# Hybrid attention layer on one core: a new order for loading, transposing and first using the token tiles

## The chip, the core and the metric

The kernel runs on 1 core of one Trainium2 chip. The metric is the device time of one execution in microseconds (us). Engines are named as in the profile: PE (TensorE matmul), PEld (its weight load), DVE (VectorE), ACT (ScalarE), POOL (GpSimd), SP (SyncE, which here only issues DMAs).

## What is computed

One layer over 512 tokens of width 1024, in float32. The index path, which the change touches first, decides for each query which 128 keys it may see.

```python
xn = rms_norm(h, norm_gain[l])
proj = xn @ w_in[l]
(q_a, k_a, v_a, g_a, q_i, k_i, w_i, c_q, c_kv, k_rope, g_b) = jnp.split(proj, offsets, axis=-1)
...
rel = jax.nn.relu(jnp.einsum('bqhd,bsd->bqhs', qib, k_idx).astype(jnp.float32))
score = jnp.einsum('bqhs,bqh->bqs', rel, wb.astype(jnp.float32)) * idx_scale
_, sel = lax.top_k(score, topk)
...
mixed = jnp.concatenate([o_a.reshape(B, S, A_WIDTH) * jax.nn.silu(g_a),
                         o_b.reshape(B, S, B_WIDTH) * jax.nn.silu(g_b)], axis=-1)
h = h + mixed @ w_out[l]
```

With 128 keys to keep, the first 128 queries see all the keys they may see, so index queries are needed for token tiles 1, 2 and 3 only.

## The kernel before

The 512 tokens are four tiles of 128. All matrix products run on pairs of tiles, a rounded part (names with h: `xh`, `wh`, `swh`) and the rest (`xl`, `wl`, `swl`), three products to a step (`mm3`, L178; recorded at L124). PE's order is written out by hand (`manual_schedule`, L88). The order on DVE, ACT, POOL and SP is made by the framework's scheduler.

The start. SP loads the four token tiles into `xin` (L196), two at a time, with the identity `ident` and three gain rows (`grow`, a `tmp` tile in the trace; L205 to L208) between them, then the small weights `smw` (L200, L201), 104 columns that make the index keys, head weights and rotary key. Per tile, ACT and DVE sum squares (L339, L340), DVE adds (L341), POOL takes the power -1/2 (`rsqrt`, L216), DVE scales the tile in place (L346). `x_turn` (L354) transposes on PE into PSUM banks and, once both tiles of a pair are in, ACT writes `xh` (L366) and DVE `xl` (L369), 256 tokens at a time. The pairs are (0, 1), then (2, 3).

Then PE makes the small projection in the bank `sm_acc` in two halves of 256 tokens (`small_step`, L476), and the index queries `q_i` of tiles 1, 2, 3 as a skewed stream (L482) woven into the second half. `use_small` (L420) turns the small projection to token-major and makes the index keys `kih`, `kil`. The latent projection `c_kv` follows, with the index scores (`sc<-kih,qi`) woven in from its tenth step on.

Weights come in chunks of 128 rows (`chunk`, L257): a DMA into one of 3 buffers `wst` (L259), a rounding copy `wh` on ACT (L263), a subtraction `wl` on POOL or DVE (L266; a string of letters such as "PPPD" says which). A chunk's DMA waits until the buffer is free, so until the `wl` three chunks earlier is done. SP issues in order. Eight counters (`DMAHW0` to `DMAHW7`) report landings and are used in turn, so an issue also waits for the landing of the DMA that was issued eight before it.

Eight small loads (`cs32`, `wide`, `gcol`, `gb`, `ga`; L487 to L492) stand in SP's order between the third and the fourth weight chunk.

Of the kernel before, what the change touches and what calls it, by code (L numbers as in the profile page):

```python
# [9 lines left out]
F32 = mybir.dt.float32  # L10
F32R = mybir.dt.float32r
# [5 lines left out]
D = 1024  # L17
# [27 lines left out]


AHEAD = 8
BANKS = {"mm": 3, "tr": 2, "sc": 2, "pv": 1}

LAG_KI = 7500  # L50
# [32 lines left out]
def layer(ctx: ExitStack, tc: tile.TileContext, x, norm_gain, w_in, a_q_norm, a_k_norm, b_q_latent,  # L83
# [21 lines left out]
    def psum(tag):  # L105
        return PS.tile([128, 512], F32, name=tag, tag=tag, bufs=BANKS[tag])

    def f32(ap):
        return ap.bitcast(F32)
# [17 lines left out]
    def transpose(o, i, idn):  # L127
        nc.tensor.transpose(o, i, idn)  # L128
        clock[0] += 107.0
# [19 lines left out]
    def run(g):  # L149
        for _ in g:  # L150
            tick()

    def take(g, n):
        for _ in range(n):
            if next(g, None) is None:
                return
            yield 1
# [20 lines left out]
    def mm3(o, lh, ll, rh, rl, first, last):  # L178
        matmul(o, lh, rh, first, False)
        matmul(o, lh, rl, False, False)  # L180
        matmul(o, ll, rh, False, last)
# [10 lines left out]
    wst = sb("qk8", (128, 8, 104), name="smw")  # L192
    wv = w_in.rearrange("(k p) c -> p k c", p=128)
    SWH, SWL = sb("V", (128, 8, 104), F32R, "swh"), sb("V", (128, 8, 104), F32R, "swl")
    for t in range(NT):
        nc.sync.dma_start(xin[t // 2][:, t % 2], xv[:, t])  # L196
        if t == NT - 1:
            for a in range(0, 8, 4):
                ks = slice(a, a + 4)
                nc.sync.dma_start(wst[:, ks, 0:32], wv[:, ks, 3272:3304])  # L200
                nc.sync.dma_start(wst[:, ks, 32:104], wv[:, ks, 2560:2632])  # L201
                nc.scalar.copy(SWH[:, ks], wst[:, ks])
                nc.gpsimd.tensor_tensor(SWL[:, ks], wst[:, ks], f32(SWH[:, ks]), op=OP.subtract)
        if t == 1:
            nc.sync.dma_start(ident, cst[:, 768:896])  # L205
            nc.sync.dma_start(grow[0:8], norm_gain.rearrange("(k p) -> k p", p=128))
            nc.sync.dma_start(grow[8:11], b_q_latent.rearrange("(k p) -> k p", p=128))
            nc.sync.dma_start(grow[11:13], b_kv_latent.rearrange("(k p) -> k p", p=128))  # L208

    nhalf = P.tile([128, 8], F32, name="nhalf")  # L210
    nc.gpsimd.memset(nhalf, -0.5)
# [6 lines left out]

    copies, subs, used = [], [], [0]

    def first(ins, m):

        for c in copies[used[0] + 1 + m:]:
            tc.add_manual_dep(c.ins, ins.ins.name, mybir.DependencyInfo(
                mybir.DependencyClass.NoSync, mybir.DependencyReason.DATA), reason="order")

    plan, where, done = [], {}, []
    IN = {"q_a": 0, "k_a": 512, "v_a": 1024, "g_a": 1536, "q_i": 2048, "g_b": 3304}
# [1 line left out]
    def weight(name, eng="P", high="A"):  # L230


        part = None
        if "/" in name:
            name, part = name.split("/")
        if name in IN:
            w, k0, k1, c, n = w_in, 0, 8, IN[name], 512
        elif name == "c_q":
            w, k0, k1, c, n = w_in, 0, 8, 2632, 384
        elif name == "c_kv":  # L240
            w, k0, k1, c, n = w_in, 0, 8, 3016, 256
        elif name[:3] == "ukv":
            w, k0, k1, c, n = w_ukv, 0, 2, 512 * int(name[3]), 512
        elif name[:2] == "uq":
            w, k0, k1, c, n = w_uq, 0, 3, 384 * int(name[2]), 384
        else:
            k0, k1 = {"ob": (4, 8), "oa": (0, 3), "oz": (3, 4)}[name[:2]]
            w, c, n = w_out, 512 * int(name[2]), 512
        ks = list(range(k0, k1))
        if part:  # L250
            a, b = part.split(":")
            ks = ks[int(a):int(b)]
        for i, k in enumerate(ks):
            where[name, k - k0] = len(plan)
            plan.append((w, k, c, n, eng[i % len(eng)], high[i % len(high)]))
# [20 lines left out]
            done.append(chunk(*plan[len(done)]))  # L276
        return done[j]

    weight("q_i", "PPPD")
    weight("c_kv", "P")  # L280
    weight("c_q", "D")
    for n in ("g_b/0:2", "ukv0", "g_b/2:3", "uq0", "g_b/3:5", "ukv1", "g_b/5:6", "uq1", "g_b/6:8"):
# [24 lines left out]
    def stream(jobs, group=2, banks=("mm",), skew=True):  # L307

        order, start = [], 0
        for i, (nk, _, _) in enumerate(jobs):  # L310
            s = start if skew else start - start % nk
            order += [(s + k, i, k) for k in range(nk)]
            start += nk / group
        acc = {}
        for _, i, k in sorted(order):
            nk, step, use = jobs[i]
            if k == 0:
                acc[i] = psum(banks[i % len(banks)])
            step(acc[i], k)
            if k == nk - 1:  # L320
                use(acc.pop(i))
            yield 1
# [6 lines left out]
    def xh(k):  # L329
        return XH[k // 4][:, k % 4]  # L330

    def xl(k):
        return XL[k // 4][:, k % 4]

    for t in range(NT):
        xt = xin[t // 2][:, t % 2]
        r = small(4)
        sq = tmp(), tmp()
        nc.scalar.activation(sq[0], xt[:, 0:512], AF.Square, scale=D ** -0.5, accum_out=r[:, 0:1])  # L339
        nc.vector.tensor_tensor_reduce(sq[1], xt[:, 512:], xt[:, 512:], 1.0 / D, EPS, OP.mult, OP.add, r[:, 1:2])  # L340
        nc.vector.tensor_tensor(r[:, 2:3], r[:, 0:1], r[:, 1:2], op=OP.add)  # L341
        rsqrt(r[:, 3:4], r[:, 2:3])
        w = D // 2 if t == NT - 1 else D
        for a in range(0, D, w):
            xs = xt[:, a:a + w]
            nc.vector.tensor_scalar(xs, xs, r[:, 3:4], None, op0=OP.mult)  # L346
    gp = psum("pv")
    transpose(gp[:, :13], grow[:13], ident[:13, :13])
    nc.scalar.copy(gains, gp[:, :13])


    xb = {}

    def x_turn(t):  # L354
        hf = t // 2
        if t % 2 == 0:
            xb[hf] = [psum(b) for b in (("tr", "tr", "sc", "sc"), ("mm", "mm", "mm", "tr"))[hf]]
        for k in range(8):
            c = (k % 2) * 256 + (t % 2) * 128
            transpose(xb[hf][k // 2][:, c:c + 128], xin[hf][:, t % 2, k * 128:k * 128 + 128], ident)  # L360
        parts = lambda k: [xb[hf][k // 2][:, (k % 2) * 256:(k % 2) * 256 + 256]] + [
            f(k)[:, hf * 256:hf * 256 + 256] for f in (xh, xl)]
        for b in range(0, 8 if t % 2 else 0, 2):
            for k in (b, b + 1):
                p, h, l = parts(k)
                nc.scalar.activation(h, p, AF.Copy, scale=gains[:, k:k + 1])  # L366
            for k in (b, b + 1):
                p, h, l = parts(k)
                nc.vector.scalar_tensor_tensor(l, p, gains[:, k:k + 1], f32(h), op0=OP.mult, op1=OP.subtract)  # L369


    cs32 = P.tile([128, 2, NT, 32], F32, name="cs32")
# [96 lines left out]
    def lat_kv(_, a):  # L469
        latent(a, 11, ckv, ckvs, "pt2")  # L470

    for t in range(NT):
        x_turn(t)
    sm_acc = psum("pv")

    def small_step(hf, k):  # L476
        c = slice(hf * 256, hf * 256 + 256)
        mm3(sm_acc[:104, c], SWH[:, k], SWL[:, k], xh(k)[:, c], xl(k)[:, c], k == 0, k == 7)

    for k in range(8):  # L480
        small_step(0, k)
    qi_ = stream(tok_jobs("q_i", 8, xh, xl, 512, [1, 2, 3], lambda t, a: use_qi(t, a)), 3, skew=True)  # L482
    for k in range(8):
        small_step(1, k)
        run(take(qi_, 1))
        if k == 2:
            nc.sync.dma_start(cs32, cst[:, 512:768])  # L487
    nc.sync.dma_start(wide, cst[:, 896:1408])
    for i, (b, a) in enumerate(((b_q_norm, a_q_norm), (b_k_norm, a_k_norm))):
        nc.sync.dma_start(gcol[0:64, 1 + i:2 + i], b[0:64].rearrange("(p o) -> p o", o=1))  # L490
        nc.sync.dma_start(gb[:, i], rows(b, 96))
        nc.sync.dma_start(ga[:, i], rows(a, 64))  # L492
    use_small(None, sm_acc)

    HALF = slice(0, 64), slice(64, 128)
# [2 lines left out]
    def use_qi(t, a):  # L500
        q = tmp()
        q3 = q.rearrange("p (h d) -> p h d", h=8)
        m = tmp((128, 8, 32))
        first(nc.scalar.copy(q, a), KEEP_QI)
        rope_mul(q3[:, :, 0:32], m, q3[:, :, 0:32], cs32, t, 8, 32)
        nc.vector.tensor_tensor(q3[:, :, 0:32], q3[:, :, 0:32], m, op=OP.add)

        def turn():
            p = psum("tr")
            for h in range(4):  # L510
                transpose(p[:, tok(h)], q[:, tok(h)], ident)
            p3 = p.rearrange("p (h c) -> p h c", h=4)
            for u in range(2):
                nc.scalar.copy(QI[u][HALF[u], :, tok(t - 1)], p3[HALF[u]])
            for u in range(2):
                a, b = QI[u][HALF[u], :, tok(t - 1)], QI[u][HALF[1 - u], :, tok(t - 1)]
                nc.vector.tensor_tensor(b, p3[HALF[u]], f32(a), op=OP.subtract)
        later(LAG_QI, turn)

    run(qi_)  # L520
    with tc.issue_after(subs[-1].ins):
# [43 lines left out]
    rl = P.tile([128, 8], F32, name="rl")  # L565

    rlx = P.tile([128, 16], F32, name="rlx")
    epsc = P.tile([128, 1], F32, name="epsc")
    nc.gpsimd.memset(epsc, EPS)
    kr = P.tile([128, NT, 32], F32, name="kr")  # L570
    kb = P.tile([128, NT], F32, name="kb")

# [367 lines left out]
```

## Time and profile before

| | us |
|---|---|
| median of 3 runs (lowest, highest) | 350.75 (348.65, 354.21) |
| the profiled execution | 350.51 |
| span of its trace, first to last instruction | 348.4 |

Times in the rows are microseconds from the start of the span. What lies around the span is 350.51 - 348.4 = 2.1 us. "idle before" in brackets is how long the engine had nothing to do, and what it waited for.

### The profile page before, as it was taken

The numbers are of one execution on the slowest core, as the hardware profiler recorded it, in microseconds if no ns is written. First come the engines' busy times: TensorE is split into PE (matmuls) and PEld (weight loads), VectorE is DVE, ScalarE is ACT, GpSimd is POOL, SyncE is SP. The second block draws the span as 40 slices with busy tenths as digits, with TensorE's granted clock in tenths as the row PEclk, the third lists the DMA queues.
The fourth block names the chain that finished last, engine by engine and source line by source line (L and its number), as shares of the span: only waits on it lengthen the run. The fifth ranks groups of instructions, "written<-read, shape, count | busy, mean of one in ns | idle before, by whom it ended". The sixth has DMA issues, their size and how long they took to land.

```text
span 348.4 us, 5497 instructions
## 1 busy us (share of the span) xinstructions
PE 328.3 (94%) x1696; PEld 273.9 (79%) x1696; DVE 264.5 (76%) x633; ACT 219.5 (63%) x528; POOL 181.7 (52%) x194
## 2 busy tenths in 40 slices
PE   2999999999999999999999799999999699999995
PEld 2887787887787888788888688888887588887884
DVE  4926787769998496887989889687997378667556
ACT  4944658583657785878876689434427688888210
POOL 1645452268689994236514379439827436356000
PEclk9999999999999999999999999999999899999999
DMA  7753334134033233013210055426678306200006
GB/s 264 192 150 105 92 115 144 31 99 122 24 105 92 74 105 94 0 32 98 83 33 0 18 135 151 122 60 152 178 188 279 111 20 201 70 16 0 2 0 241
DMA packets 28806, 34.83 MB, mean 100 GB/s; under 512 B 5341, under 2 KB 16874, under 8 KB 28778
## 3 DMA queue, kind: packets, MB, share of 16 engines
q1 hardware_dynamic: 28778, 34.49, 34.7%
q8 instruction: 13, 0.21, 0.2%
q14 instruction: 15, 0.12, 0.1%
HBM read 27.14 MB, written 2.10 MB: 84 GB/s over the span
## 4 chain that ended last, share of the span: by engine, by line
PE 64%; DVE 15%; DMA 7%; ACT 6%; issue 4%; POOL 2%; SPq 1%; DVEq 0%; ACTq 0%; POOLq 0%
PE mm L124 37%; PE sc L124 12%; PE pv L124 6%; PE tr L128 5%; DMA wst<-in_w_in 4%; DVE acc L552 2%; DVE m L551 2%; PE mm L128 2%; PE tr L124 2%; DVE ob L897 2%; ACT wh L263 2%; DMA wst<-in_w_out 1%; ACT z L683 1%; DVE z L682 1%; DMA xin<-in_x 1%
## 5 line engine op out<-in xcount | busy, mean ns | idle before, releaser
L266 POOL TENSOR_TENSOR wl<-wst,wh 128x512 fp32r<-128x512 f32 (+2 forms) x79 | 97.3, 1238 | 64.9 <-ACT wh L263 63.3
L263 ACT CAST wh<-wst 128x512 fp32r<-128x512 f32 (+2 forms) x89 | 51.7, 586 | 40.4 <-DMA wst<-in_w_in 21.3
L124 PE MATMUL mm<-wh,xh 128*128 128x512 f32 x120 | 50.3, 419 | 0.0
L124 PE MATMUL mm<-wl,xh 128*128 128x512 f32 x120 | 47.6, 396 | 0.2 <-POOL wl L266 0.2
L124 PE MATMUL mm<-wh,xl 128*128 128x512 f32 x120 | 47.4, 395 | 0.0
L216 POOL TENSOR_TENSOR sml<-sml,nhalf 128x4 f32<-128x4 f32 (+2 forms) x28 | 32.1, 1147 | 24.7 <-ACT sml L799 13.1
L683 ACT ACTIVATE z<-z,sml 128x512 f32<-128x512 f32 (+1 forms) x64 | 35.8, 560 | 9.5 <-DVE sml L682 9.1
L690 POOL TENSOR_SCALAR z<-z,sml 128x512 f32<-128x512 f32 (+2 forms) x32 | 18.8, 588 | 41.0 <-DVE sml L686 41.0
L124 PE MATMUL mm<-xh,wh 128*128 128x512 f32 x80 | 33.4, 417 | 0.0
L124 PE MATMUL mm<-xl,wh 128*128 128x512 f32 x80 | 31.7, 396 | 0.0
L124 PE MATMUL mm<-xh,wl 128*128 128x512 f32 x80 | 31.6, 395 | 0.0
L124 PEld LDWEIGHTS mm<-wh,xl 128*128 128x128 f32 x120 | 22.6, 188 | 5.4
L551 DVE MAX8 m<-acc 128x8 f32<-128x512 f32 (+2 forms) x48 | 26.4, 551 | 0.0
L552 DVE MATCH_REPLACE8 acc<-m,acc 128x512 f32<-128x512 f32 (+2 forms) x48 | 26.0, 541 | 0.0
L124 PEld LDWEIGHTS mm<-wl,xh 128*128 128x128 f32 x120 | 22.7, 189 | 3.5 <-POOL wl L266 0.5
L124 PEld LDWEIGHTS mm<-wh,xh 128*128 128x128 f32 x120 | 22.6, 189 | 3.0
L413 DVE TENSOR_TENSOR pl<-tr,ph 128x512 fp32r<-128x512 f32 (+1 forms) x32 | 17.6, 549 | 7.2 <-ACT ph L412 7.1
L124 PE MATMUL sc<-kl,bhl 96*128 96x512 f32 (+3 forms) x96 | 20.0, 320 | 0.0
L412 ACT CAST ph<-tr 128x512 fp32r<-128x512 f32 (+1 forms) x32 | 15.2, 473 | 7.7 <-PE tr L128 7.2
L128 PE MATMUL tr<-ident,z 128*128 128x128 f32 x96 | 16.1, 277 | 3.6 <-ACT z L692 3.5
L682 DVE CUSTOM_DVE_ANT_0 z<-sc,wide,nqb 128x512 f32<-128x512 f32 (+3 forms) x32 | 17.2, 541 | 2.5 <-PE sc L124 1.6
L682 DVE CUSTOM_DVE_ANT_0 z<-sc,acc,nqa 128x512 f32<-128x512 f32 (+2 forms) x24 | 14.5, 612 | 5.9 <-PE sc L124 5.7
(213 smaller groups left out, 886.6 us busy)
## 6 DMA issues: line engine op xcount, KB each, us to landing
wst<-in_w_in SPq DMA_DIRECT2D x48, 256.0 KB, 2.7
wst<-in_w_out SPq DMA_DIRECT2D x16, 256.0 KB, 2.9
xin<-in_x SPq DMA_DIRECT2D x4, 512.0 KB, 4.2
k_a<-tmp SPq DMA_DIRECT2D x16, 128.0 KB, 3.3
ob<-in_x SPq DMA_DIRECT2D x8, 256.0 KB, 3.6
out<-ob SPq DMA_DIRECT2D x7, 256.0 KB, 2.0
wst<-in_w_in SPq DMA_DIRECT2D x8, 192.0 KB, 2.6
wst<-in_w_uq SPq DMA_DIRECT2D x6, 192.0 KB, 2.2
```

The lines of the kernel that those rows point to most:

```text
L124: nc.tensor.matmul(o, l, r, start=start, stop=stop)
L128: nc.tensor.transpose(o, i, idn)
L216: nc.gpsimd.tensor_tensor(dst, src, nhalf[:, :src.shape[-1]], op=OP.pow)
L263: copies.append(nc.scalar.copy(h, st))
L266: i = E(eng).tensor_tensor(l, st, f32(h), op=OP.subtract)
L412: nc.scalar.copy(h, p)
L413: return nc.vector.tensor_tensor(l, p, f32(h), op=OP.subtract)
L551: nc.vector.max(m, masks[t])
L552: dve[0] = nc.vector.match_replace(masks[t], m, masks[t], -3e38).ins
L682: dve[0] = nc.vector.tensor_tensor_reduce(z, sc[:, :n], mask(t), nq(h, t), 3e38, OP.add, OP.min, r[:, i:i + 1]).ins
L683: nc.scalar.activation(z, z, AF.Exp, bias=r[:, i:i + 1], scale=-1.0, accum_out=r[:, 2 + i:3 + i])
L690: nc.gpsimd.tensor_scalar(z, z, w, 0.0, op0=OP.mult, op1=OP.add)
```

## The change

The identity is loaded first, then the token tiles in the order 1, 2, 3, 0; the gain rows go out from ACT's queue. PE multiplies a tile of zeros 15 times before its first transpose. The pairs are now (1, 2) and (3, 0). After the first pair is transposed and split, PE makes the index queries of tiles 1 and 2, and after each of the first four chunks of `q_i` transposes one bank of the second pair. The small projection follows in one piece of 512 tokens, woven with the other four chunks of `q_i` for tiles 1 and 2. Tile 3's index queries come last, from the same eight chunks. The small weights are loaded after the first three weight chunks, and `wide` and the others after that. The sum of the two halves' squares is added on POOL, and every tile is scaled in two halves. Two chunks of `q_i` get their `wl` on DVE, as before, but the fifth and eighth (before: the fourth and eighth).

```diff
-    for t in range(NT):
-        nc.sync.dma_start(xin[t // 2][:, t % 2], xv[:, t])
...
+    PAIRS = (1, 2), (0, 3)
+    XIN = {t: xin[i][:, j] for i, ts in enumerate(PAIRS) for j, t in enumerate(ts)}
+    nc.sync.dma_start(ident, cst[:, 768:896])
+    for t in (1, 2, 3, 0):
+        nc.sync.dma_start(XIN[t], xv[:, t])
+    nc.scalar.dma_start(grow[0:8], norm_gain.rearrange("(k p) -> k p", p=128))
...
+    zero = tmp()
+    nc.vector.memset(zero, 0.0)
+    zr = zero.bitcast(F32R)
+    warm = psum("mm")
+    for _ in range(WARM):
+        nc.tensor.matmul(warm, zr[:, 0:128], zr, start=True, stop=True)
...
-    weight("q_i", "PPPD")
+    weight("q_i", "PPPPDPPD")
...
-        nc.vector.tensor_tensor(r[:, 2:3], r[:, 0:1], r[:, 1:2], op=OP.add)
+        nc.gpsimd.tensor_tensor(r[:, 2:3], r[:, 0:1], r[:, 1:2], op=OP.add)
...
+    for t in (1, 2):
+        x_scale(t)
...
+    for j in range(2):
+        for b in range(4):
+            x_turn(0, b, j)
+            if j == 1:
+                x_split(0, b)
+    for t in (3, 0):
+        x_scale(t)
...
-    for k in range(8):
-        small_step(0, k)
-    qi_ = stream(tok_jobs("q_i", 8, xh, xl, 512, [1, 2, 3], lambda t, a: use_qi(t, a)), 3, skew=True)
-    for k in range(8):
-        small_step(1, k)
-        run(take(qi_, 1))
...
+    q1 = stream(tok_jobs("q_i", 8, xh, xl, 512, [1, 2], lambda t, a: use_qi(t, a)), 2, skew=False)
+    for b in range(4):
+        run(take(q1, 2))
+        x_bank(1, b)
+        for j in (1, 0):
+            x_turn(1, b, j)
+        x_split(1, b)
+        if b == 0:
+            for a in range(0, 8, 4):
...
+            nc.sync.dma_start(cs32, cst[:, 512:768])
...
+    sm_acc = psum("pv")
+    for k in range(8):
+        mm3(sm_acc[:104], SWH[:, k], SWL[:, k], xh(k), xl(k), k == 0, k == 7)
+        run(take(q1, 1))
+    use_small(None, sm_acc)
+    qi_ = stream(tok_jobs("q_i", 8, xh, xl, 512, [3], lambda t, a: use_qi(t, a)), 1)
+    nc.sync.dma_start(wide, cst[:, 896:1408])
```

From the latent projection on, the order on every engine is the same in both kernels, but for a few neighbours that trade places. Before it, the order differs; three places follow.

On ACT, at the start, before (`xin_63` and `xin_64` each hold two token tiles, `xh_91` the first four and `xh_92` the last four blocks of 128 features):

```order
L339 ACTIVATE tmp,sml<-xin_63 128x512 x2
L349 COPY gains<-pv 128x13
L339 ACTIVATE tmp,sml<-xin_64 128x512 x2
L366 ACTIVATE xh_91<-tr,gains 128x256 x3
L202 CAST swh<-smw 128x416
...
L366 ACTIVATE xh_92<-sc,gains 128x256 x4
...
L263 CAST wh<-wst 128x512
```

and now (`xin_63` holds tiles 1 and 2, `xin_64` tiles 0 and 3):

```order
L350 ACTIVATE tmp,sml<-xin_63 128x512 x2
L350 ACTIVATE tmp,sml<-xin_64 128x512
L390 COPY gains<-pv 128x13
L350 ACTIVATE tmp,sml<-xin_64 128x512
L381 ACTIVATE xh_101<-tr,gains 128x256 x4
L271 CAST wh<-wst 128x512 x2
L381 ACTIVATE xh_102<-sc,gains 128x256 x4
L271 CAST wh<-wst 128x512
L381 ACTIVATE xh_101<-tr,gains 128x2x128 x2
L271 CAST wh<-wst 128x512
```

The squares of all four tiles still stand ahead of the first `xh`; the first `wh` moves up to right behind four of the first pair's eight `xh`.

On PE, now, from the first instruction to the third weight chunk:

```order
L212 MATMUL mm<-tmp 128x512 x15
L130 MATMUL pv<-ident,tmp 128x13
L130 MATMUL tr<-ident,xin_63 128x128 x4
L130 MATMUL sc<-ident,xin_63 128x128 x4
...
L126 MATMUL mm<-wh,xh_101 128x512
L126 MATMUL mm<-wl,xh_101 128x512
L126 MATMUL mm<-wh,xl_103 128x512
...
L130 MATMUL tr<-ident,xin_64 128x128 x4
```

Before, all 32 transposes and 12 steps of the small projection stood ahead of the first product with `wh`; now 16 transposes stand ahead of it, and the second of its three products needs `wl` at once.

On SP, now, from the first weight chunk to the fourth (with what each issue waits for):

```order
L267 DMA wst<-in_w_in 128x512 [waits DMAHW0_49]
L267 DMA wst<-in_w_in 128x512 [waits DMAHW1_49]
L267 DMA wst<-in_w_in 128x512 [waits DMAHW2_49]
L537 DMA smw<-in_w_in 128x4x32 [waits DMAHW3_49]
L538 DMA smw<-in_w_in 128x4x72 [waits DMAHW4_49]
...
L539 DMA cs_182<-cst 128x256 [waits DMAHW7_49]
L555 DMA wide<-cst 128x512 [waits DMAHW0_49]
L557 DMA gcol<-in_b_q_norm 64x1 [waits DMAHW1_49]
...
L559 DMA ga<-in_a_k_norm 128x64 [waits DMAHW6_49]
L267 DMA wst<-in_w_in 128x512 [waits DMAHW7_49,Pool_49]
```

The three chunks now go out behind the token tiles, and the four loads of `smw` stand between them and the fourth chunk together with the eight small loads; counter 3 is the landing of tile 3, counter 4 that of tile 0, the last.

## Rows read from the trace of the kernel before

**Rows 1.** The page: busy time by engine, and the chain that ended last.
```profile
PE 328.3 (94%) x1696; PEld 273.9 (79%) x1696; DVE 264.5 (76%) x633; ACT 219.5 (63%) x528; POOL 181.7 (52%) x194
...
PE 64%; DVE 15%; DMA 7%; ACT 6%; issue 4%; POOL 2%; SPq 1%; DVEq 0%; ACTq 0%; POOLq 0%
```

**Rows 2.** Timeline of PE, start to first index scores: start, us, engine, line, what.
```profile
6.93 1.11 PE L128 MATMUL tr<-ident,xin 128*128 128x128 f32 x4 [0.70 <-DVE xin L346]
...
13.66 0.36 PE L124 MATMUL pv<-xh,swh 128*104 128x256 f32 x1
...
16.93 0.40 PE L124 MATMUL mm<-wh,xh 128*128 128x512 f32 x1
17.17 0.39 PE L124 MATMUL mm<-wl,xh 128*128 128x512 f32 x1
...
19.62 0.51 PE L124 MATMUL mm<-wl,xh 128*128 128x512 f32 x1 [0.19 <-POOL wl L266]
...
34.93 0.63 PE L128 MATMUL tr<-ident,tmp 128*128 128x128 f32 x4 [0.51 <-DVE tmp L506]
...
38.21 0.60 PE L128 MATMUL tr<-ident,tmp 128*128 128x128 f32 x4
38.56 0.49 PE L124 MATMUL pv<-xh,wh 128*128 128x512 f32 x1
38.89 0.40 PE L124 MATMUL pv<-xl,wh 128*128 128x512 f32 x1
...
42.33 0.65 PE L128 MATMUL tr<-ident,tmp 128*128 128x128 f32 x4 [0.27 <-DVE kil L413]
...
47.03 0.40 PE L124 MATMUL sc<-kih,qi 128*128 128x512 f32 x1
```

**Rows 3.** Timeline of DVE: the first and the last token tile arrive.
```profile
4.10 0.69 DVE L340 CUSTOM_DVE_ANT_0 tmp<-xin 128x512 f32<-128x512 f32 x1 [4.10 <-DMA xin<-in_x]
...
9.15 0.69 DVE L340 CUSTOM_DVE_ANT_0 tmp<-xin 128x512 f32<-128x512 f32 x1 [0.50 <-DMA xin<-in_x]
```

**Rows 4.** Timeline of ACT and POOL: square, split, weight copy, weight subtraction.
```profile
9.23 0.63 ACT L339 ACTIVATE tmp<-xin 128x512 f32<-128x512 f32 x1 [1.23 <-DMA xin<-in_x]
...
9.86 1.18 ACT L366 ACTIVATE xh<-tr,gains 128x256 fp32r<-128x256 f32 x3
...
11.72 1.58 ACT L366 ACTIVATE xh<-sc,gains 128x256 fp32r<-128x256 f32 x4
...
18.98 0.62 ACT L263 CAST wh<-wst 128x512 fp32r<-128x512 f32 x1 [0.78 <-DMA wst<-in_w_in]
...
18.28 1.29 POOL L266 TENSOR_TENSOR wl<-wst,wh 128x512 fp32r<-128x512 f32 x1 [0.88 <-ACT wh L263]
```

**Rows 5.** Timeline of SP: the small weights, the eight small loads, the fourth chunk.
```profile
5.92 0.51 SPq L200 DMA_DIRECT2D smw<-in_w_in  x1
...
9.94 0.43 SPq L487 DMA_DIRECT2D cs<-cst  x1
...
13.85 0.33 SPq L492 DMA_DIRECT2D ga<-in_a_k_norm  x1
16.17 18.69 SPq L259 DMA_DIRECT2D wst<-in_w_in  x13
```

**Rows 6.** DMA issues of the first 20 us: KB each, us from issue to landing.
```profile
smw<-in_w_in SPq DMA_DIRECT2D x2, 144.0 KB, 4.7
```

**Rows 7.** PE after its longest later wait: timeline, then windows (PEclk: granted clock).
```profile
272.73 0.66 PE L128 MATMUL tr<-ident,z 128*128 128x128 f32 x4 [3.00 <-ACT z L692]
...
274.00:276.00 2.00, 2.00 (x9) 1.89 (x8) 0.57 (x3) 1.92 (x6) 1.22 (x2) 0.50 0.51 173
276.00:278.00 2.00, 2.00 (x8) 1.55 (x8) 1.11 (x3) 0.69 (x3) 0.00 (x0) 0.70 0.46 145
```

**Rows 8.** PEld: four transposes early and four late in the first stage.
```profile
7.62 0.87 PEld L128 LDWEIGHTS sc<-ident,xin 128*128 128x128 f32 x4
...
12.03 0.42 PEld L128 LDWEIGHTS mm<-ident,xin 128*128 128x128 f32 x4
```

More of the change, by code (lines that the diff above doesn't have):

```diff
@@ L47 @@
 AHEAD = 8
+WARM = 15
 BANKS = {"mm": 3, "tr": 2, "sc": 2, "pv": 1}
@@ L194, in layer @@
     SWH, SWL = sb("V", (128, 8, 104), F32R, "swh"), sb("V", (128, 8, 104), F32R, "swl")
-    for t in range(NT):
-        nc.sync.dma_start(xin[t // 2][:, t % 2], xv[:, t])
[L197 to L208, printed above, removed]
+    PAIRS = (1, 2), (0, 3)
[4 more added lines that the diff above has]
+    nc.scalar.dma_start(grow[0:8], norm_gain.rearrange("(k p) -> k p", p=128))
+    nc.scalar.dma_start(grow[8:11], b_q_latent.rearrange("(k p) -> k p", p=128))
+    nc.scalar.dma_start(grow[11:13], b_kv_latent.rearrange("(k p) -> k p", p=128))
+    zero = tmp()
[4 more added lines that the diff above has]
+        nc.tensor.matmul(warm, zr[:, 0:128], zr, start=True, stop=True)
     nhalf = P.tile([128, 8], F32, name="nhalf")
@@ L219, in layer, with after @@
     copies, subs, used = [], [], [0]
+    def after(v, u):
+        tc.add_manual_dep(v.ins, u.ins.name, mybir.DependencyInfo(
+            mybir.DependencyClass.NoSync, mybir.DependencyReason.DATA), reason="order")
     def first(ins, m):
         for c in copies[used[0] + 1 + m:]:
-            tc.add_manual_dep(c.ins, ins.ins.name, mybir.DependencyInfo(
-                mybir.DependencyClass.NoSync, mybir.DependencyReason.DATA), reason="order")
+            after(c, ins)
     plan, where, done = [], {}, []
@@ L333, in xl, with x_scale @@
         return XL[k // 4][:, k % 4]
-    for t in range(NT):
-        xt = xin[t // 2][:, t % 2]
+    epsc = P.tile([128, 1], F32, name="epsc")
+    nc.gpsimd.memset(epsc, EPS)
+    def x_scale(t):
+        xt = XIN[t]
         r = small(4)
@@ L340, in layer, with x_bank, x_turn, x_split @@
         nc.vector.tensor_tensor_reduce(sq[1], xt[:, 512:], xt[:, 512:], 1.0 / D, EPS, OP.mult, OP.add, r[:, 1:2])
-        nc.vector.tensor_tensor(r[:, 2:3], r[:, 0:1], r[:, 1:2], op=OP.add)
+        nc.gpsimd.tensor_tensor(r[:, 2:3], r[:, 0:1], r[:, 1:2], op=OP.add)
         rsqrt(r[:, 3:4], r[:, 2:3])
[L343 to L346, printed above, removed]
+        for a in (0, 512):
+            nc.vector.tensor_scalar(xt[:, a:a + 512], xt[:, a:a + 512], r[:, 3:4], None, op0=OP.mult)
+    xb, xsp = {}, {}
+    def x_bank(i, b):
+        if b == 0:
+            xb[i] = {}
+        xb[i][b] = psum(("tr", "tr", "sc", "sc")[b])
+    def x_turn(i, b, j):
+        for k in (2 * b, 2 * b + 1):
+            c = (k % 2) * 256 + j * 128
+            transpose(xb[i][b][:, c:c + 128], XIN[PAIRS[i][j]][:, k * 128:k * 128 + 128], ident)
+    def x_split(i, b):
+        def parts(k):
+            p = xb[i][b][:, (k % 2) * 256:(k % 2) * 256 + 256]
+            h, l = xh(k), xl(k)
+            if i == 0:
+                return p, h[:, 128:384], l[:, 128:384]
+            return [p.rearrange("p (j c) -> p j c", j=2)] + [
+                v.rearrange("p (t c) -> p t c", t=NT)[:, 0:NT:3] for v in (h, l)]
+        for k in (2 * b, 2 * b + 1):
+            p, h, l = parts(k)
+            xsp[i, b] = nc.scalar.activation(h, p, AF.Copy, scale=gains[:, k:k + 1])
+        for k in (2 * b, 2 * b + 1):
+            p, h, l = parts(k)
+            nc.vector.scalar_tensor_tensor(l, p, gains[:, k:k + 1], f32(h), op0=OP.mult, op1=OP.subtract)
+    for t in (1, 2):
+        x_scale(t)
     gp = psum("pv")
@@ L349, in layer @@
     nc.scalar.copy(gains, gp[:, :13])
[L352 to L357, printed above, removed]
-        for k in range(8):
[L359 to L369, printed above, removed]
+    for b in range(4):
+        x_bank(0, b)
+    for j in range(2):
[5 more added lines that the diff above has]
+        x_scale(t)
     cs32 = P.tile([128, 2, NT, 32], F32, name="cs32")
@@ L470, in lat_kv @@
         latent(a, 11, ckv, ckvs, "pt2")
[L472 to L478, printed above, removed]
-    for k in range(8):
-        small_step(0, k)
-    qi_ = stream(tok_jobs("q_i", 8, xh, xl, 512, [1, 2, 3], lambda t, a: use_qi(t, a)), 3, skew=True)
-    for k in range(8):
-        small_step(1, k)
-        run(take(qi_, 1))
[L486 to L493, printed above, removed]
     HALF = slice(0, 64), slice(64, 128)
@@ L518, in use_qi @@
         later(LAG_QI, turn)
+    q1 = stream(tok_jobs("q_i", 8, xh, xl, 512, [1, 2], lambda t, a: use_qi(t, a)), 2, skew=False)
+    for b in range(4):
+        run(take(q1, 2))
[3 more added lines that the diff above has]
+        x_split(1, b)
+        if b == 0:
+            for a in range(0, 8, 4):
+                ks = slice(a, a + 4)
+                nc.sync.dma_start(wst[:, ks, 0:32], wv[:, ks, 3272:3304])
+                nc.sync.dma_start(wst[:, ks, 32:104], wv[:, ks, 2560:2632])
+            nc.sync.dma_start(cs32, cst[:, 512:768])
+    for a in range(0, 8, 4):
+        ks = slice(a, a + 4)
+        c = nc.scalar.copy(SWH[:, ks], wst[:, ks])
+        after(c, xsp[1, 1])
+        i = nc.gpsimd.tensor_tensor(SWL[:, ks], wst[:, ks], f32(SWH[:, ks]), op=OP.subtract)
+    for v in copies[5:]:
+        after(v, c)
+    for v in subs[4:]:
+        after(v, i)
+    sm_acc = psum("pv")
[5 more added lines that the diff above has]
+    nc.sync.dma_start(wide, cst[:, 896:1408])
+    for i, (b, a) in enumerate(((b_q_norm, a_q_norm), (b_k_norm, a_k_norm))):
+        nc.sync.dma_start(gcol[0:64, 1 + i:2 + i], b[0:64].rearrange("(p o) -> p o", o=1))
+        nc.sync.dma_start(gb[:, i], rows(b, 96))
+        nc.sync.dma_start(ga[:, i], rows(a, 64))
     run(qi_)
@@ L567, in layer @@
     rlx = P.tile([128, 16], F32, name="rlx")
-    epsc = P.tile([128, 1], F32, name="epsc")
-    nc.gpsimd.memset(epsc, EPS)
     kr = P.tile([128, NT, 32], F32, name="kr")
```

## The prediction

> **What bounds the kernel now.** I read the page first. PE is busy 94% of the span and carries 64% of the chain that ended last [rows 1]: the kernel is a queue of products, so an edit pays when it brings PE's queue forward or takes a wait out of it. The change edits the time up to the latent projection, so next comes PE's timeline there [rows 2]. PE does nothing before 6.93 us. It transposes until 13.66, where the small projection starts, makes its first product with a weight at 16.93, the first of the latent projection at 38.56, the first index score at 47.03. After 13.66 it waits seldom: 0.35 us at 19.62, where a `wl` is late (19.27, one product after the last, would have been its turn), some 0.5 at 34.93, 0.27 at 42.33. So what the stage can give back lies before 13.66 and is about 7 us of transposing with waits in it.
>
> Since PE's, ACT's, DVE's and POOL's orders are practically equal in both kernels from the latent projection on, I compare two instants: the first product of the latent projection (38.56 before) and the first index score (47.03 before). A shift there goes through to the end, because PE stays the bound.
>
> **The work of PE between the first weight product and the latent projection.** Successive products of 512 columns start 0.235 us apart (16.93 to 17.17) [rows 2]. The changed order has 72 of them for the index queries and 24 for the small projection: 96 x 0.235 = 22.6. A group of four transposes among them costs 0.45: 0.35 to the next product (38.21 to 38.56) and 0.1 more until that one has passed (0.33 instead of 0.235, 38.56 to 38.89) [rows 2]. There are seven: four of the pair (3, 0), one of the small projection, two of index queries; 3.15. Together 25.7 us.
>
> **When the first weight product can start.** Tiles landed from 4.10 to 9.15 before [rows 3]. Four tiles of 512 KB still have to come, now with the identity ahead and no small weights queued right behind. I take 9.0 for the last one, tile 0, with ends of 8.6 and 9.5. The order of ACT decides the rest: the square of tile 0 stands ahead of the first `xh`, so no `xh` begins before about 9.0 + 0.63 = 9.63 [rows 4]. Four `xh` at 1.58 for four and one weight copy of 0.62 follow: the first `wh` is there at 9.63 + 1.58 + 0.62 = 11.8 [rows 4], and PE makes its first weight product at 11.8 instead of 16.93. Its second needs `wl`, 1.29 on POOL [rows 4]: there at 13.1, while PE would have had its turn at 12.05. A new wait of 1.05 us; behind it on PE stands everything, the transposes of tiles 3 and 0 too.
>
> **The fourth chunk.** After that wait PE needs 5 x 0.235 for the first chunk, 1.41 for each of the next two (POOL's 1.29 per chunk keeps pace) and 0.45 for each of three groups of transposes: 13.1 + 1.2 + 2.8 + 1.35 = 18.45, and the second product of the fourth chunk would have its turn at 18.7. Its DMA stands behind four loads of small weights, of which the second waits for tile 0 (9.0), and the eight small loads. Issues of small weights take 0.5 each, the eight took 9.94 to 14.18, or 4.24 [rows 5]. So it goes out at 9.0 + 3 x 0.5 + 4.24 = 14.75, though its buffer is free at 13.1. It lands 2.8 later as its predecessor did (issue 16.17, copy begun 18.98) [rows 4, 5]: 17.55; copy and subtraction make `wl` ready at 17.55 + 0.62 + 1.29 = 19.45. A second wait, 0.75 us. The ends: none, if the issues go faster by that much; 2.2 us, if the later small loads have to wait for the small weights' landings eight issues earlier (4.7 us from issue [rows 6], so 13.7 for the second, 15.2 until all are out) and the last tile is late too. After that chunk PE meets no late weight: two `q_i` steps now last 2.8 us per chunk beside the small projection, and the third tile reuses chunks that are there.
>
> **The sum.** First product of the latent projection: 11.8 + 25.7 + 1.05 + 0.75 = 39.3, or 0.7 later than 38.56. From there to the first index score 8.47 us passed before, for ten steps of 0.705 and two groups of transposes, 7.95, and waits of 0.5, of which the 0.27 before `kil` is the largest seen [rows 2]. Now the index keys' transposes stand later in PE's queue and ought to find them ready: 0.5 back. Net +0.2 us. Added to the profiled execution, 350.51, that gives 350.7, which is also the median of the runs, 350.75.
>
> **Edits that I cost at nothing.** The zeros: 15 products, at most 2 x 0.235 us each at half pace, end by about 8, and at full pace by 5; tile 1 can be transposed at about 7 and ACT takes it at 9.63, so even the slower end hides behind the last tile. The memset ahead of them runs on DVE, idle until 4.10 [rows 3]. The gain rows on ACT's queue and ACT's table load are over before the first tile lands. The sum of squares on POOL is not in the trace in this form; whether it takes 0.2 or the 0.56 of POOL's power, it delays DVE's scaling by under half a microsecond, and tile 2's scaling has about one to spare against ACT's wait for tile 0. Without that cover it would cost the same half microsecond. The full-rate transposes that the zeros may buy lie under the same wait.
>
> [...]
>
> **The rivals.**
> 1. The clock falls. Now PE has nothing to do from about 9.3 (tile 2 transposed) to 11.8, makes one product and waits again. [...] Against it: the zeros and transposes lie close before. [...]
> 2. The start is quicker than I think. The tiles end at 8.6, since nothing of small packets follows them, and the fourth chunk goes out while its predecessor is still being used: 0.4 + 0.75 off, and perhaps another microsecond where later stages use the earlier index keys: 348.5 to 349.5. For it: PE and ACT both wait for tiles up to 9.15 [rows 3, 4], and a load leaves that stretch. Against it: ACT's order ties all to tile 0.
> 3. Slower: SP is the bound. If each small load waits for small weights that land 5 us or more after issue, the fourth chunk goes out at 16 to 17 instead of 14.75, the fifth and sixth right behind it, and PE waits 2 to 3 us at one place: 352.5 to 353.5. It decides from a late issue of more than a microsecond on; to be slower by over 2% (7 us) the weight stream would have to stay behind for the whole latent projection, which the eight chunks in store there speak against.
> 4. Nothing at the start matters because the index path sets the end anyway. Then the later small projection would show as PE waiting at the first index score; I find only 0.7 us to spare there: the keys' transposes come after seven steps and one group, at 39.3 + 4.95 + 0.45 = 44.7, and take 0.45, a copy 0.62 and a DVE pass of that width 0.69 [rows 3, 4], so `kil` is there at 46.5, against 39.3 + 7.95 = 47.25. A miss would cost 0.5 to 1: 351.5.
>
> **How the numbers follow.** No shift worth measuring, within a microsecond: 0.4. Clock: 0.25. Quicker: 0.2. SP's queue: 0.1. Index keys late: 0.05. All of these lie within 2% of 350.75, which is about what a measurement of this kernel can tell from no change; I leave 0.03 for faster and 0.04 for slower by more, for a later stage that locks in differently. The range takes in rivals 1 to 3, and the runs themselves lie 2 to 3 us apart: 347.3 to 353.4.
>
> **What would show it.** Right: first product with a weight near 11.8, a wait for `wl` of about 1 us behind it, another of up to 1 us at the fourth chunk, the fourth chunk issued near 14.75, the latent projection at 39 to 39.5, the first score at 47 to 47.5. Wrong: a granted clock of 0.50 between 12 and 18 (rival 1); the first weight product before 11 with no wait at the fourth chunk (rival 2); an issue after 16 (rival 3); a wait before the first score (rival 4).

## The result, and the profile after

| | before | after |
|---|---|---|
| median, us (lowest, highest; 4 runs each) | 351.23 (348.65, 354.21) | 356.19 (354.03, 356.59) |
| profiled execution / its span | 350.51 / 348.4 | 354.03 / 352.2 |

The ratio is 1.0131, 95% interval 1.0083 to 1.018: slower by 1.3%, less than 2%, but 5.0 us where 0.2 were forecast, and 356.19 lies above the range's end of 353.4. Ratios, here and below, leave out the runs of a kernel that took over 1.5% more than its fastest; one run of e8, at 414.66 us, lies farthest off.

The page after, against [rows 1]: busy time per engine, the granted clock in 40 slices, the chain.

```profile
PE 334.0 (95%) x1687; PEld 277.0 (79%) x1687; DVE 264.3 (75%) x633; ACT 218.8 (62%) x528; POOL 184.0 (52%) x198
...
PEclk9899999998799999999999999999999999999999
...
PE 65%; DVE 9%; issue 8%; DMA 6%; POOL 5%; ACT 4%; SPq 1%; POOLq 0%; DVEq 0%; ACTq 0%
```

Nothing there names the loss: PE is the bound as before. The clock has two dents, in the second slice (9 to 18 us) and at 79 to 97 us. PE's timeline after, against [rows 2] (start, duration, line, tiles; in brackets the idle time before and its releaser):

```profile
1.45 5.00 PE L212 MATMUL mm<-tmp 128*128 128x512 f32 x15 [1.45 <-DVE tmp L208]
...
11.79 0.50 PE L126 MATMUL mm<-wh,xh 128*128 128x512 f32 x1 [1.57 <-ACT wh L271]
13.23 0.50 PE L126 MATMUL mm<-wl,xh 128*128 128x512 f32 x1 [0.94 <-POOL wl L274]
...
20.55 0.50 PE L126 MATMUL mm<-wh,xh 128*128 128x512 f32 x1 [0.20 <-ACT wh L271]
21.90 0.50 PE L126 MATMUL mm<-wl,xh 128*128 128x512 f32 x1 [0.85 <-POOL wl L274]
...
39.24 0.66 PE L130 MATMUL tr<-ident,tmp 128*128 128x128 f32 x4 [0.73 <-ACT sm L458]
...
42.53 0.40 PE L126 MATMUL pv<-xh,wh 128*128 128x512 f32 x1
...
50.32 0.39 PE L126 MATMUL sc<-kih,qi 128*128 128x512 f32 x1
51.33 0.50 PE L126 MATMUL sc<-kil,qi 128*128 128x512 f32 x1 [0.62 <-DVE kil L443]
```

The start is as forecast: first weight product 11.79, its `wl` at 13.23. What follows is not: the fourth chunk's `wl` is used at 21.90 (forecast 19.45), the latent projection begins at 42.53 (39.3) and the first score at 50.32 (47.2), 3.29 later than before. ACT's and SP's timelines, against [rows 4, 5], and the DMA view of the first 24 us (busy share in tenths, 0.6 us per digit; then one load, with its KB and us from issue to landing), against [rows 6]:

```profile
9.04 0.63 ACT L350 ACTIVATE tmp<-xin 128x512 f32<-128x512 f32 x1 [0.49 <-DMA xin<-in_x]
...
11.11 1.15 ACT L271 CAST wh<-wst 128x512 fp32r<-128x512 f32 x2
...
19.88 0.62 ACT L271 CAST wh<-wst 128x512 fp32r<-128x512 f32 x1 [3.47 <-DMA wst<-in_w_in]
```

```profile
9.17 1.66 SPq L539 DMA_DIRECT2D cs<-cst  x1
...
14.19 0.43 SPq L559 DMA_DIRECT2D ga<-in_a_k_norm  x1
14.73 15.02 SPq L267 DMA_DIRECT2D wst<-in_w_in  x9
```

```profile
DMA  0005895999999999999999310031057994000088
...
ga<-in_a_k_norm SPq DMA_DIRECT2D x1, 32.0 KB, 5.0
```

The last tile comes at 9.04 and the fourth chunk goes out at 14.73, as forecast to 0.05 us. But ACT copies that chunk at 19.88, 5.15 later; the same chunk took 2.8 before [rows 4, 5]. Meanwhile the DMA engines are nearly idle (digits 3, 1, 0, 0, 3, 1, 0 from 13.2 us): the chunk's data moves only from about 17.4 us on. Ahead of it in SP's queue stand the eight small loads, the last issued at 14.19 and landing 5.0 later, at 19.2. Before, the chunk went out 2 us after the last of them.

Windows after, against [rows 7] (length, busy time of PE, PEld, DVE, ACT and POOL with counts, granted clock, DMA share, GB/s):

```profile
14.00:16.00 2.00, 2.00 (x9) 1.73 (x8) 1.82 (x5) 0.68 (x3) 1.86 (x2) 0.63 0.15 35
16.00:18.00 2.00, 2.00 (x6) 1.42 (x6) 0.88 (x2) 0.41 (x2) 0.00 (x0) 0.52 0.28 56
18.00:20.00 2.00, 2.00 (x14) 1.68 (x13) 0.00 (x0) 0.12 (x1) 0.00 (x0) 1.00 0.87 334
...
86.00:88.00 2.00, 2.00 (x9) 1.81 (x10) 2.00 (x8) 0.00 (x0) 0.39 (x2) 0.55 0.68 181
88.00:90.00 2.00, 2.00 (x7) 1.52 (x6) 2.00 (x8) 0.00 (x0) 1.57 (x1) 0.50 0.21 81
90.00:92.00 2.00, 2.00 (x6) 1.61 (x5) 1.93 (x7) 0.92 (x4) 0.63 (x1) 0.50 0.00 0
```

The granted clock fell to 0.63 and 0.52 behind the gap at the start (2 x 0.37 + 2 x 0.48 = 1.7 us) and again to 0.55, 0.50 and 0.50 at 86 us (2 x 0.45 + 2 x 0.50 + 2 x 0.50 = 2.9 us in the three windows shown), behind a wait of 0.64 and 16 products of one column. The second fall is not in every execution of the changed kernel: e5 below lacks it (1.00 from 82 to 94). Nor does it need the changed order: e6, which keeps before's order there, has it (0.53 and 0.62 from 86 to 90). The two traces of before don't (1.00).

Three theories. A: the fourth chunk's transfer waits behind the small loads and sets the time. B: the clock's fall at 14 to 18 us does. C: the zeros, which raised the clock early only to lose it, are at fault.

### The profile page after: what moved, and what is told of

The parts are those of the page before. It is cut to its first block, busy times and chain, and to the rows that moved or that the text cites. A ratio compares the mean times of both kernels' runs of the same rounds, so it can differ in the third digit from the quotient of the medians.

```text
span 352.2 us, 5492 instructions
## 1 busy us (share of the span) xinstructions
PE 334.0 (95%) x1687; PEld 277.0 (79%) x1687; DVE 264.3 (75%) x633; ACT 218.8 (62%) x528; POOL 184.0 (52%) x198
## 4 chain that ended last, share of the span: by engine, by line
PE 65%; DVE 9%; issue 8%; DMA 6%; POOL 5%; ACT 4%; SPq 1%; POOLq 0%; DVEq 0%; ACTq 0%
PE mm L126 35%; PE sc L126 12%; PE pv L126 7%; PE tr L130 5%; DMA wst<-in_w_in 4%; POOL wl L274 3%; PE tr L126 2%; PE mm L130 2%; DVE ob L936 2%; DMA xin<-in_x 1%; DMA wst<-in_w_out 1%; ACT z L722 1%; DVE acc L593 1%; DVE m L592 1%; DVE z L721 1%
## 5 line engine op out<-in xcount | busy, mean ns | idle before, releaser
L271 ACT CAST wh<-wst 128x512 fp32r<-128x512 f32 (+2 forms) x89 | 51.3, 585 | 39.1 <-DMA wst<-in_w_in 19.2
L126 PE MATMUL mm<-wh,xh 128*128 128x512 f32 x120 | 51.1, 426 | 1.8 <-ACT wh L271 1.8
L126 PEld LDWEIGHTS sc<-kl,bhl 96*128 96x128 f32 x96 | 16.6, 189 | 2.9
```

The source lines that it names most:

```text
L126: nc.tensor.matmul(o, l, r, start=start, stop=stop)
L271: copies.append(nc.scalar.copy(h, st))
```

## The experiments

All times below are from 3 rounds (the last: 5) against the kernel before on the same chip. For each kernel's profiled execution: first weight product, `wl` of the fourth chunk where PE waited for it, latent projection, first score, and the rest of the span behind that score; then the medians of all runs, of the kernel and of before beside it, and the ratio (in e2 it rests on two runs, so it carries little). The row e1 sets the kernel before against itself: the medians differ by 1.8 us without any edit.

| kernel | first weight | 4th `wl` | latent | score | rest | medians | ratio (95%) |
|---|---|---|---|---|---|---|---|
| before | 16.93 | none | 38.56 | 47.03 | 301.4 | 351.23 | 1 |
| e1 before again | 16.90 | none | 38.26 | 46.73 | 300.5 | 354.15 / 352.38 | 0.9991 (0.9927, 1.0055) |
| after | 11.79 | 21.90 | 42.53 | 50.32 | 301.9 | 356.19 / 351.23 | 1.0131 (1.0083, 1.018) |
| e5 after again | 12.37 | 22.71 | 44.91 | 52.74 | 304.5 | 356.33 / 352.04 | 1.0156 (1.0075, 1.0236) |
| e2 small loads late | 12.66 | none | 40.24 | 48.07 | 304.8 | 353.00 / 352.38 | 0.9873 (0.9749, 0.9997) |
| e3 gap filled | 13.33 | 22.53 | 43.16 | 51.00 | 301.2 | 354.62 / 352.38 | 1.0058 (1.0007, 1.0109) |
| e4 both | 13.37 | none | 40.41 | 48.24 | 302.2 | 350.66 / 352.38 | 0.9881 (0.9803, 0.996) |
| e6 zeros in before | 20.65 | none | 41.11 | 49.58 | 302.8 | 354.63 / 352.04 | 1.0004 (0.9947, 1.0061) |
| e7 chunk ahead of tile 0 | 12.51 | none | 41.40 | 49.28 | 302.8 | 353.85 / 352.04 | 1.0058 (1.0018, 1.0098) |
| e8 the same, wait filled | 11.75 | none | 39.74 | 47.62 | 300.5 | 350.06 / 352.04 | 0.9963 (0.9921, 1.0004) |
| e9 no zeros | 11.86 | 24.60 | 46.81 | 54.61 | 304.4 | 358.33 / 353.59 | 1.0166 (1.0093, 1.024) |
| e10 all | 13.21 | none | 38.97 | 46.92 | 302.9 | 349.78 / 353.59 | 0.9932 (0.9889, 0.9976) |

**The two kernels again** (e1, e5, no edit).

> The kernel before, unchanged, profiled once more. The changed kernel's trace shows a second fall of the granted clock, to 0.50 at 86 to 93 us, behind the 16 one-column products of the latent scales; the first trace of the kernel before passes the same place at full clock. If that fall is chance, this trace or the clocks of these runs show it too in some executions (means near 0.985 beside 0.995, times 3 us apart). If it belongs to the change, every run here has a clock of 0.99 or more and the trace keeps 1.00 from 80 to 95 us.

> The changed kernel, unchanged, profiled once more. If the clock's fall behind the start is the rule there, it falls again between 12 and 20 us; if it is chance, as the second one at 86 to 93 us, this trace may pass either place at full clock. In either case the fourth chunk is issued between 14.5 and 15.5, its subtraction ends near 22, and the first index score comes at 50 to 51 (before: 46.7 to 47.0 in two traces).

The loss repeats. In this execution of after the clock stayed up at 86 us (1.00) but fell at 204 (0.57) and 278 (0.50); in that of before only at 272 (0.50). So the later falls come and go between executions of one kernel, 1.6 to 3.4 us each, and go with much of the spread of the runs (before: 348 to 357 us): of e1's ten runs the two at a mean granted clock of 0.995 took 349.3 and 350.5, the two at 0.981 355.8 and 356.9. The late fourth chunk repeats (issued 15.28, copied 20.69); so does the fall at the start (0.78, 0.50 and 0.87 from 12 to 18 us), and a further one at 22 to 28 us (0.84, 0.50, 0.81) lies behind that chunk.

**Small loads late** (e2): `cs32` goes out behind the fifth chunk of weights, `wide` and the other six behind the seventh.

```diff
+            with tc.issue_after(dmas[4].ins):
+                nc.sync.dma_start(cs32, cst[:, 512:768])
...
+    with tc.issue_after(dmas[6].ins):
+        nc.sync.dma_start(wide, cst[:, 896:1408])
```

> The changed kernel with the eight small loads moved on SP behind the fifth and the seventh weight chunk. Theory of two brakes (late fourth chunk and fallen clock, each hiding part of the other): the fourth chunk goes out at about 13.2 us instead of 14.73, its subtraction ends near 18 instead of 21.85, PE's two waits at that chunk (0.20 and 0.85) are gone, the clock still falls at 14 to 18; first product of the latent projection at about 41.2 instead of 42.53. Rival (only the clock counts): it stays at 42.5.

SP's and ACT's timelines of e2, then its DMA view of the first 24 us:

```profile
14.07 1.78 SPq L267 DMA_DIRECT2D wst<-in_w_in  x2
```

```profile
16.78 0.62 ACT L271 CAST wh<-wst 128x512 fp32r<-128x512 f32 x1
```

```profile
DMA  0005899775899999999994000976786728978841
```

The chunk now takes 2.7 us from issue to copy, and the engines carry its data from 15.0 us, 0.9 after issue instead of 2.7. PE does not wait for it. The latent projection comes 27.58 after the first weight product, not 30.74. So the small loads held the transfer up, as A has it; which of the eight did was not tried. The clock did not fall at 12 to 18 here (1.00), though the gap was left as it was (idle 1.57 and 0.94 around the first product), so this run took the late chunk and the fall away together; the next one parts them. The second fall (0.50 from 84 to 90) is in this trace too.

**The gap filled** (e3): 24 zero products of 240 columns between the first pair's transposes and the first weight product.

```diff
+    fill(psum("mm"), 24)
     for b in range(4):
         run(take(q1, 2))
```

> The changed kernel with 24 products of zeros (240 columns) between the transposes of the first pair and the first weight product, so that PE has no gap from 10.2 to 13.2 us. Both theories: granted clock 1.00 from 14 to 18 instead of 0.63 and 0.52. Two brakes: the fourth chunk's subtraction still ends near 21.9, so PE only waits longer there and the latent projection still starts at 42.3 to 42.6. Only the clock counts: 40.9, 1.6 us earlier.

```profile
16.00:18.00 2.00, 2.00 (x13) 1.64 (x13) 0.88 (x2) 0.84 (x2) 0.67 (x1) 1.00 0.19 44
18.00:20.00 2.00, 1.77 (x10) 1.25 (x8) 0.00 (x0) 0.00 (x0) 0.00 (x0) 1.00 0.81 304
20.00:22.00 2.00, 0.51 (x1) 0.19 (x1) 0.10 (x1) 1.50 (x4) 0.80 (x1) 1.00 0.25 96
```

The windows show the clock at 1.00, and PE idle for 1.7 us of 18 to 22 instead. The `wl` of the fourth chunk is used at 22.53, and the latent projection follows 20.63 later, to the hundredth as in after (42.53 - 21.90). So B falls for the start, and A is left: the fall at 14 to 18 lies wholly in front of a chunk that is late anyway. Behind the chunk it does cost: e5 and e9 fell again there (0.50 in one window each) and took 22.2 for the same stretch.

**Both** (e4: the edits of e2 and e3).

> Both edits of the two runs before together. Two brakes: latent projection at 39.4 to 39.8, about 3 us earlier than in the changed kernel, so more than the sum of the two alone; the whole about 353 if the second fall of the clock stays, 350 if it goes. Only the clock counts: 40.9, as with the zeros alone.

From first weight product to latent projection 27.04, half a microsecond under e2. At 40.41 it misses what was expected: the last tile landed at 9.81 instead of 9.04, and a wait of 0.73 remained, ahead of the index queries' transposes that follow those of the small projection.

**The zeros alone, in the kernel before** (e6).

> The kernel before with the 15 products of zeros alone. If transposes at full pace are worth something by themselves, the small projection starts before 13.66 us, by up to 1 us; if the token tiles and DVE set that instant, it starts at 13.5 to 13.7 as before and the time is that of before within 0.3%.

```profile
10.87 0.87 PE L128 MATMUL mm<-ident,xin 128*128 128x128 f32 x6 [0.81 <-DVE xin L353]
14.95 0.66 PE L128 MATMUL tr<-ident,xin 128*128 128x128 f32 x2 [3.21 <-DVE xl L376]
```

The small projection starts at 16.97, later than either expectation, with a fall at 14 to 18 us here too (0.61, 0.54). But PE's timeline shows a wait of 3.21 us that before doesn't have, for `xl`, which empties a bank. The zeros have an `mm` bank of their own, and the transposes of the second pair use `mm` banks; that the one pushed the other back was not tried. So this run tells nothing of the zeros alone.

**The first chunk ahead of tile 0's square** (e7: e2, and `copies[0]`, `subs[0]` put ahead of tile 0's square and sum).

```diff
+    wt("q_i", 0)
...
+        if t == 0:
+            after(s0, copies[0])
+            after(add, subs[0])
```

> The changed kernel with the small loads late, and the first weight chunk's copy ahead of tile 0's square on ACT and its subtraction ahead of tile 0's sum on POOL. If the start is set by ACT's and POOL's order around tile 0, the wait of 0.94 us for the first subtraction goes and the latent projection starts 1.5 to 2 us earlier than with the late small loads alone (27.6 us after the first weight product there), first score at 46 to 46.7, the whole 1 us under before. If the tiles' landing sets it, nothing moves by more than 0.5.

It missed: the first weight product stayed at 12.51, since the copy came to stand behind four `xh`, which began at 10.39; the wait for its `wl` stayed too (0.86); and the clock fell at 12 to 18 (0.88, 0.50, 0.77). With that fall and no late chunk to hide it the stretch took 28.89, 1.3 over e2.

**The same, with the wait near 270 us filled** (e8: e7, the small projection's transposes a group sooner, 20 zero products ahead of the transposes near 270).

```diff
-LAG_SMALL = 2500
+LAG_SMALL = 1200
...
+            if not turn and not PT:
+                fill(p, 20)
```

> The run before this one, with the small projection's transposes two steps earlier (so that the last index queries' transposes need not wait 0.73 us for them) and 20 products of zeros in PE's wait of 2.6 to 3.0 us near 270 us. Where PE is kept busy through that wait the granted clock stays 1.00 from 268 to 284 us, which saves 1.6 us in the executions in which it falls there; the start saves 0.7. About 348 to 349, against 350.5 of the run before this one.

No wait of 0.73 ahead of the index queries' transposes, and no fall between 268 and 284 (1.00). One trace without that fall shows little, since after and e3 have none there either; but of the ten traces without these zeros eight have it, of the two with them (e8, e10) neither. The rest, 300.5, is as short as e1's, where that fall is. Nine of its ten runs lie between 348.44 and 352.53.

**No zeros** (e9: after with `WARM = 0`).

> The changed kernel without the 15 zero products (their number set to 0), nothing else. My theory is that the zeros together with the thin stretch behind them make the fall of the clock at 12 to 18 us, since the same zeros put alone into the kernel before had one there (0.61 and 0.54) and the kernel before without them none. Then the windows from 12 to 18 stand at 1.00 here. The latent projection gains less than the 1.7 us of the clock, because the fourth chunk, which lands about 5 us after its issue, is then what PE waits for (as with the filled gap, where nothing was gained): first weight product 11.8 to 12.6, wait at the fourth chunk 1.5 to 3, latent projection 42 to 43.5. Rival: the thin stretch alone makes the fall (four transposes, one product, a wait): a granted clock near 0.5 to 0.6 at 14 to 18 also here, latent projection 42.5 to 44. Ratio to before by either: 1.005 to 1.015.

PE's timeline and a window of e9:

```profile
7.33 1.11 PE L130 MATMUL tr<-ident,xin 128*128 128x128 f32 x4 [2.01 <-DVE xin L355]
...
14.65 0.63 PE L126 MATMUL mm<-wl,xh 128*128 128x512 f32 x1
15.08 0.63 PE L126 MATMUL mm<-wh,xl 128*128 128x512 f32 x1
...
24.60 0.51 PE L126 MATMUL mm<-wl,xh 128*128 128x512 f32 x1 [2.40 <-POOL wl L274]
```

```profile
14.00:16.00 2.00, 2.00 (x7) 1.50 (x7) 2.00 (x5) 1.03 (x3) 1.46 (x2) 1.00 0.11 32
```

The window says 1.00, as my theory had it, but products start 0.43 apart until 18.5, the pace that after shows at a granted clock of 0.52: without the zeros PE started at half pace here (0.43 instead of the 0.23 from 19.47 to 20.64) and the granted clock didn't report it; in [rows 8] too four weight loads took 0.87 us early and 0.42 late, both at a granted clock of 1.00. So C falls: without the zeros the first weight products ran at half pace too, until 18.5 (in after from about 15 to 18), and the first came no sooner (11.86); the zeros gained a pace (two groups of transposes start 0.49 us apart in after, 0.90 here) that was lost again in after behind the thin stretch. The latent projection came at 46.81, outside both expectations, with a fall at 24 to 30 (0.87, 0.50, 0.78) in it: POOL here took the small weights (20.78, 2.10 us) ahead of the fourth `wl`, so that PE waited 2.40 us.

**All parts** (e10: e4, with e8's lag and filled wait).

> The changed kernel with the small loads late, the 24 zero products in the gap before the first weight product, the small projection's transposes one product group sooner (their lag 2500 to 1200) and 20 zero products in PE's wait near 270 us. By my theory the gains of the parts add: latent projection at 39.5 to 40 (40.41 without the shorter lag, less 0.73), no fall of the clock at 12 to 18 nor at 272 to 282, so about 1.5 us under the version without the last two parts on the average over executions: a median of 348.5 to 350.5, ratio 0.985 to 0.993, with only the falls near 84 to 92 and 200 to 206 left to differ between executions. Rival: the falls that are taken away come back at a later thin stretch, and PE is bound by its products: ratio 0.993 to 1.000, a median of 350.5 to 352.

PE's timeline of e10:

```profile
13.21 0.39 PE L126 MATMUL mm<-wh,xh 128*128 128x512 f32 x1
13.75 0.50 PE L126 MATMUL mm<-wl,xh 128*128 128x512 f32 x1
...
38.97 0.40 PE L126 MATMUL pv<-xh,wh 128*128 128x512 f32 x1
```

The latent projection comes 25.76 after the first weight product, with only 0.3 of waiting in it (13.75 instead of 13.45): the 25.7 of PE work that the prediction counted. Its 12 runs lie between 346.59 and 352.92, the interval of the ratio wholly below 1: it is faster than before by 0.7%, and so than the changed kernel, whose two ratios to before are 1.0131 and 1.0156. The parts' gains add at the start (38.97, half a microsecond better than expected); over the whole span the ratio is at the border of the two expectations, and falls at 82 to 86 (0.67, 0.50) and 198 to 202 (0.69, 0.50) were in its trace, as the rival had it.

## Why the prediction was wrong

- **PE as the bound, and that a shift at the first score goes through:** right, as far as the traces can tell. The rest behind the first score is 300.5 to 304.8 us in all twelve profiled executions, whatever the start; nothing in the order behind it was changed but by e8 and e10.
- **First weight product 11.8, wait for `wl`:** right, 11.79 and 13.23; ACT's order set it, as argued. The 9.0 for tile 0 was lucky: it fits this trace (9.04), but in e2 to e5, e9 and e10 ACT starts on that tile at 9.63 to 9.91, past the end of 9.5 that I gave.
- **PE work of 25.7:** right; e10 shows 25.76 nearly without waits.
- **The fourth chunk: the step that failed.** "It lands 2.8 later as its predecessor did" was sized on a load issued 2 us after the small ones. Issued right behind them it took 5.15, 5.41 in e5 and 2.7 with them out of the way (e2). I bounded only the issue time; the transfer had no upper end. That is 2.45 us: `wl` at 21.90 instead of 19.45. The issue time, 14.75, came out right (14.73) by two errors that cancel. The second load of small weights does not wait for tile 0, as the section on the change and the prediction have it: it goes out at 5.59, and the first issue behind that tile is `cs32`, at 9.17 instead of 10.5. From there the eight took 5.45 us (to 14.62) instead of 4.24.
- **Latent projection 39.3:** 42.53. The 2.45, and 0.73 for a wait that I hadn't listed: the index queries' transposes at 39.24 now come right behind the small projection's (37.98) and meet ACT still reading those out (`sm`). The shorter lag takes it away (e8, e10). 39.3 + 2.45 + 0.73 = 42.5.
- **Half a microsecond back before the first score:** right for the first score (7.79 from the latent projection, 8.47 before), but its second product waits 0.62 for `kil`, where 0.27 had been lost one place earlier. So the shift, 3.29 at the first score, is 4.07 at the second product (51.33 against 47.26), and the spans differ by 3.8. This is **rival 4** in small: its 0.7 to spare for `kil` took ACT and DVE as free, but ACT first made two `qi` (from 47.32 on) and a `wh`, so that `kih` began at 49.05, and DVE reached `kil` at 50.58.
- **Rival 1, the clock falls:** it fell and cost 1.7 us; the fall behind the wait of 3.00 us in [rows 7] had cost 2 x 0.50 + 2 x 0.30 = 1.6. The late chunk swallowed all of it, not only the 0.75 of the second wait forecast there. The gap alone does not decide it: e2 had the same one and kept 1.00. **Rival 3, SP late:** its price (2 to 3 us at one place) came, by a slow transfer and not by a late issue. I gave them chances as alternatives; they came together, and the range ended where either alone would. **Rival 2, a quicker start,** is in no trace: ACT takes the last tile no earlier than 9.04, and that small packets behind the tiles had held them is not shown.
- **What is left:** 3.29 us of the 5.0 are in the profiled execution's start; in e5 it was 5.7 (with the second fall at 22 to 28). The median lies between. Whether the later stages also fall oftener in the changed kernel these few traces don't settle: the rest behind the score varies by 4 us in all. The runs' mean granted clocks don't ask for it: 0.981 over the eight runs of the changed kernel and 0.990 over the 61 of before beside the experiments are some 3 us of full clock apart (0.009 x 352), and the falls at the start alone are 1.7 in after and 3.4 in e5.

## What to carry to other kernels

When a load is moved right behind a run of small ones, price its transfer behind them (here 5.2 us instead of 2.8), not its issue alone; a big load that PE waits for goes ahead of small ones that nobody needs yet (2.7 in e2). What zero products at the start win can be lost in a thin stretch between them and the first real products (after, e5, e7 and e8 fell to 0.50 to 0.52 there, e2 stayed at 1.00), and a fall that is kept away wins nothing where a late load stands behind it (e3). Before pricing a slow stretch, look for the next wait behind it: what ends there is paid once.

## What was not expected of the hardware

In after the load behind eight small ones (0.2 to 256 KB) began to move 2.7 us after its issue, while the DMA engines moved 35 to 56 GB/s (14 to 18 us); with the small ones out of the way (e2) it took 0.9. The granted clock read 1.00 over products that started 0.43 us apart (e9, 14 to 18.5 us; 0.23 from 19.47 to 20.64), so pace is read from the starts of products as well.
